# Requesting the out-projection's attention-half weights before the retention's first keys and values

## The chip, the cores and the metric

The kernel runs on one core of a Trainium2 chip. A core has five engines with instruction queues of their own: PE (TensorE, matrix products; PEld in the profile is its loading of weights), DVE (VectorE), ACT (ScalarE), POOL (GpSimd) and SP (SyncE, which here only requests transfers). Sixteen DMA engines move data between the main memory (HBM) and the core's memory (SBUF); transfers are requested by SP and ACT. The metric is the device time of one execution in microseconds (us), lower is better.

## The reference

The program is one layer of a diffusion backbone over 2048 latent tokens (a grid of 32 rows and 64 columns) of width 1024, with 256 context tokens in front. Cut to its core:

```python
h = rmsnorm(x) * (1 + scale) + shift            # scale, shift, gate from SiLU(c) @ w_ada
na_q, na_k, na_v, na_g, r_q, r_k, r_v, r_g = split(h @ w_in)      # latent and context tokens
y_na  = neighbourhood_attention(na_q, na_k, na_v, context, bias) * silu(na_g)   # 8 heads of 64
y_ret = head_rmsnorm(o_forward + o_backward) * silu(r_g)          # 4 heads of 128, chunks of 128
out   = rmsnorm(x + gate * (concat(y_na, y_ret) @ w_out))
```

The retention is computed in chunks: each chunk of 128 tokens gives a state k^T (w v), 128 by 128, where w are decay weights; states are chained forward for one direction and backward for the other. All products of large size are made from numbers split in a high and a low part (three products in place of one), to keep the precision of float32 at a higher rate.

## The kernel before

The kernel runs in stages that overlap on PE: the adaLN vectors and the in-projection; the neighbourhood attention in 128 tiles (8 heads of 16 tiles), between whose products PE does the remaining in-projection steps; then the backward states of the retention (`back_stream`); then the retention's outputs together with the out-projection. What a stage produces goes to HBM (stores, requested by ACT in this part) and is read back by a later one (requests of SP).

Each engine runs its instructions in the order in which the code is written; no scheduler reorders them. The code around the change is written in this order. After the last attention tile, `flush()` issues the stores that are still deferred, among them the last head's y (yS<-y, line 151, on ACT). The attention's memory is given back (`atx.close()`), and `tail_open` (called right then) lays the new pools over it: `wn` first, with two tiles `won0` and `won1` of 16 KB in each of the 128 partitions, then `rp` with the states, then `tb` with three buffers each of keys k4, values v4 and weighed values vw. `won0` lies where the attention's keys were; `won1` lies over the last keys' second half, the context values, the queries and the values. A new tile waits for the last reader or writer of what lay there.

`won0` and `won1` hold the high and low parts of the half of the gated out-projection weights that the attention's y is multiplied with (1024 columns, 512 rows, as four blocks of 128 rows). They are computed earlier and lie in HBM as `woS`. `load_wo(key, k)` requests block k of both: two transfers of 128 by 1024 numbers, 512 KB each. PE reads them first at the beginning of the out-projection (line 1463).

`back_stream` goes through 24 steps: for each of the 4 heads twice the context's two chunks (forward and backward; both share one load), then 16 steps of four chunks. In a step, `ahead(n)` requests the keys and values of step n + 2 (line 1175) and weighs those of step n + 1 on ACT (line 1181); `states` makes one product of 128 by 128 per chunk on PE (line 1187; a float32 product is two instructions on PE); DVE adds it into the chain of states (lines 1217 to 1224). Keys, values and weighed values have three buffers each, so the keys of step n + 3 are requested when the products of step n have read theirs (in the eight context steps, where two steps share a load, correspondingly less often). Between the steps PE makes `fill(8)`, then `fill(3)` or, from the eleventh step on, `fill(2)` steps of the in-projection that were held back: three matmuls for a k-slice, lines 374 and 363. Their outputs are rotated on DVE (lines 402 to 404, 438, 439) with tables (rot) that SP loads too, or copied by ACT (line 449), and stored by ACT (line 151). Before this change, blocks 0 to 3 of the weights are requested at the steps 2, 5, 8 and 11.

A transfer signals its landing on one of eight counters (DMAHW0 to DMAHW7), given out by the program in turn over the requests of SP and ACT. Before an engine requests a transfer on a counter, it waits until the previous transfer on it has landed. So a request can wait for an old transfer that has nothing to do with its data, and all later requests of that engine wait with it.

Of the kernel before, what the change touches and what calls it, by code (L numbers as in the profile page):

```python
# [82 lines left out]
def hybrid_kernel(ctx: ExitStack, tc: tile.TileContext, a: dict, out: bass.AP):  # L83
# [1065 lines left out]
            H["sb"] = rp.tile([P, NCH, P], F32, name=f"sb{H['r']}")  # L1149
        rt["won"] = [wn.tile([P, 4, D], F32R, name=f"won{hl}") for hl in range(2)]  # L1150

    def load_wo(key, k):
        for hl in range(2):
            nc.sync.dma_start(f(rt[key][hl])[:, k % 4, :], woS[hl][k])

    def ret_tables(H):
# [13 lines left out]
    def load_kv(p, H, n0, nn):  # L1170
        r = H["r"]
        res = []
        for src, nm in ((rkS, "k4"), (rvS, "v4")):
            t = p.tile([P, 4, P], F32, name=nm, bufs=4 if nm == "v4" and p is not rt["tb"] else 3)
            nc.sync.dma_start(t[:, :nn, :], src[r // 2][:, r % 2, n0:n0 + nn, :])
            res.append(t)
        return res

    def weigh(p, H, v4, nn, d):
        vw = p.tile([P, 4, P], F32, name="vw")  # L1180
        nc.scalar.activation(vw[:, :nn, :], v4[:, :nn, :], AF.Copy, scale=H["w"][:, d:d + 1])
        return vw

    def states(k4, vw, nn):
        t = ptile(rt["pq"]).rearrange("p (n d) -> p n d", n=4)
        for e in range(nn):
            nc.tensor.matmul(t[:, e, :], k4[:, e, :], vw[:, e, :], start=True, stop=True)  # L1187
        return t

    def back_stream():  # L1190
        rp = rt["rp"]
        back = [(H, NCH, 2, d) for H in HS for d in range(2)]
        back += [(H, 4 * n4, 4, 1) for hp in (HS[2:], HS[:2]) for n4 in range(3, -1, -1) for H in hp]
        kv, vw = {}, {}

        def ahead(n):
            if n + 2 < len(back):
                H, n0, nn, d = back[n + 2]
                kv[n + 2] = kv[n + 1] if n0 == NCH and d == 1 else load_kv(rt["tb"], H, n0, nn)
            if 0 <= n + 1 < len(back):  # L1200
                H, n0, nn, d = back[n + 1]
                vw[n + 1] = weigh(rt["tb"], H, kv[n + 1][1], nn, d)

        ahead(-2)
        ahead(-1)
        yield 1
        for n, (H, n0, nn, d) in enumerate(back):
            ahead(n)
            if n in (2, 5, 8, 11):
                load_wo("won", n // 3)  # L1210
            w, sb = H["w"], H["sb"]
            t = states(kv.pop(n)[0], vw.pop(n), nn)
            if n0 < NCH:
                for e in range(3, -1, -1):
                    m_ = n0 + e
                    if m_ > 0:
                        nc.vector.scalar_tensor_tensor(sb[:, m_ - 1, :], sb[:, m_, :], w[:, 3:4], t[:, e, :], ALU.mult, ALU.add)
            elif d == 0:
                H["sf"] = rp.tile([P, P], F32, name=f"sf{H['r']}", bufs=2)
                nc.vector.tensor_copy(H["sf"], t[:, 0, :])  # L1220
                nc.vector.scalar_tensor_tensor(H["sf"], H["sf"], w[:, 2:3], t[:, 1, :], ALU.mult, ALU.add)
            else:
                nc.vector.tensor_copy(sb[:, NCH - 1, :], t[:, 1, :])
                nc.vector.scalar_tensor_tensor(sb[:, NCH - 1, :], sb[:, NCH - 1, :], w[:, 3:4], t[:, 0, :], ALU.mult, ALU.add)
            yield 1
# [71 lines left out]
    pax.close()  # L1297
    tail_open()
    back = back_stream()
    next(back)  # L1300
    fill(8)
# [194 lines left out]
    for s in range(NJ + 3):  # L1496
        q = plan[s]
        part = [q // 4 + (q % 4 > n) for n in range(4)]
        tick()
        if s >= 4 and s % 4 == 3:  # L1500
            ready.append(s)
        if s + 1 < NJ:
            r_load(J[s + 1])
        if s in (1, 3, 5, 6):
            load_wo("wor", 4 + s // 2)
        if s == 4:
            nc.sync.dma_start(fg, a["final_g_rep"])
        if s == 6:
            nc.gpsimd.tensor_scalar(fg, fg, float(D) ** 0.5, 0.0, ALU.mult, ALU.add)
        if 0 <= s - 3 < NJ:  # L1510
            r_d(J[s - 3])
        if s < NJ:
            r_a(J[s])
        fill(part[0])
        if 0 <= s - 1 < NJ:
            r_b(J[s - 1])
        fill(part[1])
        if 0 <= s - 3 < NJ:
            r_e(J[s - 3])
        fill(part[2])  # L1520
        if 0 <= s - 2 < NJ:
            r_c(J[s - 2])
        fill(part[3])
# [98 lines left out]
```

## Time and profile before

| | before |
|---|---|
| time, median of 3 runs | 1360.26 us (1356.26 to 1361.77) |
| the profiled execution | 1357.68 us, span of its instructions 1355.7 us |
| PE busy | 1310.1 us, 97% |
| PE weight loads | 1146.9 us, 85% |
| DVE, ACT, POOL busy | 61%, 45%, 43% |
| DMA | 287.25 MB, mean 212 GB/s |

The profile is of one execution. Busy time is the time in which an engine had an instruction in work; matmuls are pipelined and their ends are modelled, so a busy PE can still be slowed. The chain of waits follows the work that ended last backwards, at each step to what released it. An SP row (SPq) is a request: its length is the time to issue it, not the transfer. "Idle before" in square brackets is the time for which the engine stood still before an instruction, with what ended it.

### The profile page before, as it was taken

The page shows a single profiled execution, that of the slowest core. Times are in us where ns is not written, and L with a number is a line of the kernel's source. Part 1 is how long each engine was busy: PE and PEld are TensorE (multiplying, and loading weights), DVE is VectorE, ACT ScalarE, POOL GpSimd, SP SyncE. Part 2 cuts the span into 40 slices and gives each one's busy share as a digit, 9 for nine tenths or more (in the row PEclk, how much of TensorE's full clock was granted, in tenths as well). Part 3 has the DMA queues.
Part 4 walks back from the last instruction along what each step waited for, and adds up shares of the span by engine and source line. Part 5 has one row for each costly group of instructions (what it writes and reads, how often), then busy time and mean ns, then how long its engine had stood idle before and what let it go on. Part 6 is the DMA issues. An engine that isn't in the chain of part 4 may idle for free.

```text
span 1355.7 us, 23094 instructions
## 1 busy us (share of the span) xinstructions
PE 1310.1 (97%) x8236; PEld 1146.9 (85%) x8236; DVE 828.3 (61%) x1444; ACT 606.5 (45%) x1259; POOL 579.9 (43%) x569
## 2 busy tenths in 40 slices
PE   6999999999999999999999999999999899999997
PEld 2477899887897788998999889889999789888886
DVE  5687366676766755377767777776654633445345
ACT  4454343343533344455555465556643244333432
POOL 4443101554034664445535474655523154544442
PEclk9999999999999999999999999999999999999999
DMA  9386788464867656978587886666528888555433
GB/s 363 135 279 231 259 313 215 164 210 147 326 182 230 216 203 213 265 210 211 148 225 207 226 224 206 195 181 193 163 90 291 278 290 279 159 163 171 163 121 129
DMA packets 172085, 287.25 MB, mean 212 GB/s; under 512 B 17345, under 2 KB 92225, under 8 KB 170690
## 3 DMA queue, kind: packets, MB, share of 16 engines
q1 hardware_dynamic: 139554, 228.35, 55.8%
q10 hardware_dynamic: 32416, 57.42, 11.8%
q8 instruction: 66, 1.08, 0.3%
q14 instruction: 49, 0.40, 0.1%
HBM read 194.48 MB, written 91.23 MB: 211 GB/s over the span
## 4 chain that ended last, share of the span: by engine, by line
PE 70%; DVE 9%; DMA 8%; POOL 4%; issue 4%; ACT 3%; SPq 1%; ACTq 0%; DVEq 0%; POOLq 0%
PE mm L374 17%; PE mm L671 12%; PE mm L1463 11%; PE mm L363 7%; PE sS L1025 4%; PE tr L1052 3%; PE po L1073 3%; PE mm L1187 2%; PE mm L311 2%; PE tr L1054 2%; PE po L1075 2%; DMA v<-rvS 1%; PE mm L1375 1%; POOL hlo L531 1%; PE mm L1374 1%
## 5 line engine op out<-in xcount | busy, mean ns | idle before, releaser
L374 PE MATMUL mm<-whi,hlo 128*128 128x256 f32 x832 | 228.6, 282 | 1.0 <-DMA hlo<-cS 1.0
L374 PE MATMUL mm<-whi,hhi 128*128 128x256 f32 x768 | 224.3, 292 | 0.0
L374 PE MATMUL mm<-wlo,hhi 128*128 128x256 f32 x768 | 216.8, 282 | 0.0
L1056 ACT CAST pt<-tr 128x640 fp32r<-128x640 f32 (+1 forms) x128 | 95.6, 747 | 160.4 <-PE tr L1054 157.8
L1062 DVE TENSOR_TENSOR pt<-tr,pt 128x640 fp32r<-128x640 f32 (+1 forms) x128 | 114.0, 890 | 78.4 <-ACT pt L1056 77.2
L374 PEld LDWEIGHTS mm<-whi,hlo 128*128 128x128 f32 x832 | 156.6, 191 | 1.4 <-DMA hlo<-cS 1.3
L1045 POOL TENSOR_SCALAR sp<-sp,stt 128x640 f32<-128x640 f32 (+2 forms) x128 | 103.1, 808 | 106.3 <-DVE stt L1044 75.7
L374 PEld LDWEIGHTS mm<-whi,hhi 128*128 128x128 f32 x768 | 146.3, 191 | 0.0
L374 PEld LDWEIGHTS mm<-wlo,hhi 128*128 128x128 f32 x768 | 146.1, 190 | 0.0
L1034 DVE CUSTOM_DVE_ANT_0 sp<-sS,nb 128x640 f32<-128x640 f32 (+2 forms) x128 | 105.6, 825 | 33.4 <-DMA nb<-in_rpb_t_dram 20.7
L1039 ACT ACTIVATE sp<-sp,stt 128x640 f32<-128x640 f32 (+2 forms) x128 | 107.4, 839 | 20.3 <-DVE stt L1034 19.1
L625 POOL TENSOR_TENSOR whi<-st,whi 128x512 fp32r<-128x512 f32 x48 | 62.8, 1330 | 107.7 <-ACT whi L624 107.7
L363 PE MATMUL mm<-hhi,whi 128*128 128x512 f32 x256 | 108.2, 423 | 0.0
L363 PE MATMUL mm<-hlo,whi 128*128 128x512 f32 x256 | 102.0, 399 | 6.0 <-DVE hlo L265 2.1
L1025 PE MATMUL sS<-k,q 128*128 128x256 f32 (+3 forms) x512 | 99.1, 315 | 5.1 <-DVE stt L1034 4.7
L363 PE MATMUL mm<-hhi,wlo 128*128 128x512 f32 x256 | 102.0, 398 | 0.3 <-DVE wlo L347 0.3
L671 PE MATMUL mm<-hhi,whi 128*128 128x512 f32 x336 | 98.1, 395 | 1.6 <-POOL whi L625 1.6
L1463 PE MATMUL mm<-wor,y 128*128 128x512 f32 x384 | 95.7, 398 | 1.1 <-DVE xt L1472 1.1
L1472 DVE TENSOR_TENSOR xt<-mm,xt 128x512 f32<-128x512 f32 x64 | 43.9, 687 | 82.6 <-PE mm L1463 82.5
L1025 PEld LDWEIGHTS sS<-k,q 128*128 128x128 f32 x512 | 82.8, 188 | 12.0 <-DVE stt L1034 8.2
L1463 PE MATMUL mm<-won,y 128*128 128x512 f32 x336 | 89.9, 406 | 0.0
L625 POOL TENSOR_TENSOR wlo<-st,wlo 128x512 fp32r<-128x512 f32 x36 | 53.1, 1476 | 75.8 <-ACT wlo L624 73.7
(258 smaller groups left out, 3051.5 us busy)
## 6 DMA issues: line engine op xcount, KB each, us to landing
st<-in_w_in_dram SPq DMA_DIRECT2D x64, 512.0 KB
q<-qS SPq DMA_DIRECT2D x64, 256.0 KB
hlo<-hS SPq DMA_DIRECT2D x20, 512.0 KB
k<-kS SPq DMA_DIRECT2D x16, 576.0 KB
kS<-o SPq DMA_DIRECT2D x16, 512.0 KB
vB<-o SPq DMA_DIRECT2D x64, 128.0 KB
qS<-o ACTq DMA_DIRECT2D x16, 512.0 KB
woS<-g ACTq DMA_DIRECT2D x32, 256.0 KB
```

Of the source, the lines that this page charges most:

```text
L363: nc.tensor.matmul(pm[:, :n], ww[:, k, cs], h[:, k, :], start=(k == 0 and i == 0), stop=(k == KC - 1 and i == 2))
L374: nc.tensor.matmul(pm[:, t * WG:(t + 1) * WG], h[:, k, o:o + P], ww[:, k, :], start=(k == 0 and i == 0), stop=(k == KC - 1 and i == 2))
L625: nc.gpsimd.tensor_tensor(t[:, 1], r, f(t)[:, 0], ALU.subtract)
L671: nc.tensor.matmul(pm, ww[:, k, :], hh[:, k, :], start=(k == 0 and i == 0), stop=(k == KH - 1 and i == 2))
L1025: nc.tensor.matmul(o, hd["q"][i][:, hl, j * P:(j + 1) * P], k, start=(hl == 0), stop=(hl == 1))
L1034: nc.vector.tensor_tensor_reduce(T["sp"][:, :n], T["s"], nbz[big][:, o:o + n], -1.0, 3e38, ALU.add, ALU.min, T["st"][:, 0:1])
L1039: nc.scalar.activation(sp[:, :n], sp[:, :n], AF.Exp, bias=st[:, 0:1], scale=-1.0, accum_out=st[:, 1:2])
L1045: nc.gpsimd.tensor_scalar(sp[:, :n], sp[:, :n], st[:, 2:3], 0.0, ALU.mult, ALU.add)
L1056: nc.scalar.copy(pt[:, :ng_ + 2, 0, :], tr[:, :ng_ + 2, :])
L1062: nc.vector.tensor_tensor(pt[:, :n, 1, :], tr[:, :n, :], f(pt)[:, :n, 0, :], ALU.subtract)
L1463: nc.tensor.matmul(pm, yy[:, k, :], ww[:, k, sl], start=(k == 0 and i == 0), stop=(k == 3 and i == 2))
L1472: nc.vector.tensor_tensor(xts[t][:, sl], pm, xts[t][:, sl], ALU.add)
```

## The change

All eight requests are taken out of the steps 2, 5, 8 and 11 and placed before the first `ahead`: the four blocks of the high parts first, then the four of the low parts.

```diff
-    def load_wo(key, k):
-        for hl in range(2):
+    def load_wo(key, k, hls=(0, 1)):
+        for hl in hls:
             nc.sync.dma_start(f(rt[key][hl])[:, k % 4, :], woS[hl][k])
...
+        for hl in range(2):
+            for k in range(4):
+                load_wo("won", k, (hl,))
         ahead(-2)
         ahead(-1)
         yield 1
         for n, (H, n0, nn, d) in enumerate(back):
             ahead(n)
-            if n in (2, 5, 8, 11):
-                load_wo("won", n // 3)
```

Only SP's list differs. Before, on SP at the end of attention (k, v: keys and values; rot: rotary tables; the names in brackets are what the request waits for: a counter, or a count of an engine's instructions):

```order
L392 DMA rot<-in_rot_k_dram 128x512 [waits DMAHW4_49]
L1175 DMA k_10725<-rkS_77 128x256 [waits DMAHW1_49,DVE_49,PE_49]
L1175 DMA v_10727<-rvS_79 128x256 [waits DMAHW3_49,DMAHW2_49,Pool_49]
L392 DMA rot<-in_rot_k_dram 128x512
L1175 DMA k_10798<-rkS_77 128x256 [waits DMAHW4_49]
L1175 DMA v_10800<-rvS_79 128x256 [waits DMAHW5_49,DMAHW6_49,DMAHW0_49,DVE_49]
L392 DMA rot<-in_rot_k_dram 128x512
L1175 DMA k_10867<-rkS_78 128x256 [waits DMAHW7_49]
L1175 DMA v_10869<-rvS_80 128x256
L1154 DMA won_10723<-woS_91 128x1024 [waits DMAHW1_49]
L1154 DMA won_10724<-woS_92 128x1024 [waits DMAHW3_49]
```

In this list the second values (v_10800) wait for counter 0, whose last holder is ACT's store of the last y. After the change, at the same place on SP:

```order
L392 DMA rot<-in_rot_k_dram 128x512 [waits DMAHW4_49]
L1154 DMA won_10723<-woS_91 128x1024 [waits DMAHW0_49,PE_49]
L1154 DMA won_10723<-woS_91 128x1024 [waits DMAHW1_49]
L1154 DMA won_10723<-woS_91 128x1024 [waits DMAHW3_49]
L1154 DMA won_10723<-woS_91 128x1024 [waits DMAHW4_49]
L1154 DMA won_10724<-woS_92 128x1024 [waits DMAHW5_49,PE_49]
L1154 DMA won_10724<-woS_92 128x1024 [waits DMAHW6_49]
L1154 DMA won_10724<-woS_92 128x1024 [waits DMAHW7_49]
L1154 DMA won_10724<-woS_92 128x1024 [waits DMAHW0_49]
L1175 DMA k_10733<-rkS_77 128x256 [waits DMAHW1_49,DVE_49]
L1175 DMA v_10735<-rvS_79 128x256 [waits DMAHW2_49,Pool_49]
L392 DMA rot<-in_rot_k_dram 128x512 [waits DMAHW3_49]
```

The eight weight requests (won_10723 high, won_10724 low) now stand ahead of the first keys and values. The count of PE that the first of them waits for is that of the last score product (line 1025); that of the fifth is the last value product (line 1075). The counters have shifted by eight places: counter 2, which the first values (v_10735) take, was held before by ACT's store of the last y.

## Rows read from the trace of the kernel before

**Rows 1.** The page: the chain that ended last, by engine

```profile
PE 70%; DVE 9%; DMA 8%; POOL 4%; issue 4%; ACT 3%; SPq 1%; ACTq 0%; DVEq 0%; POOLq 0%
```

**Rows 2.** The chain in order of time, 1040 to 1097: start, length, what

```profile
1040.89 6.21 DMA v<-rvS
...
1049.59 7.29 DMA v<-rvS
...
1069.04 5.37 DMA v<-rvS
...
1082.84 14.00 PE mm L1463 x59
```

**Rows 3.** Timeline of PE, state products (L1187): start, length, then the idle time

```profile
1039.39 1.05 PE L1187 MATMUL mm<-vw,k 128*128 128x128 f32 x8
...
1045.39 1.05 PE L1187 MATMUL mm<-vw,k 128*128 128x128 f32 x8
...
1050.37 1.05 PE L1187 MATMUL mm<-vw,k 128*128 128x128 f32 x8
1052.65 1.05 PE L1187 MATMUL mm<-vw,k 128*128 128x128 f32 x8
1057.76 1.16 PE L1187 MATMUL mm<-vw,k 128*128 128x128 f32 x8 [2.67 <-ACT vw L1181]
...
1072.11 1.05 PE L1187 MATMUL mm<-vw,k 128*128 128x128 f32 x8
1075.30 1.16 PE L1187 MATMUL mm<-vw,k 128*128 128x128 f32 x8 [0.74 <-ACT vw L1181]
...
1079.98 1.05 PE L1187 MATMUL mm<-vw,k 128*128 128x128 f32 x8
```

**Rows 4.** Timeline of SP: requests from 1012 to 1056

```profile
1012.31 0.33 SPq L1175 DMA_DIRECT2D k<-rkS  x1
...
1017.65 0.32 SPq L1175 DMA_DIRECT2D v<-rvS  x1
...
1038.27 1.91 SPq L1154 DMA_DIRECT2D won<-woS x2
...
1046.89 0.38 SPq L1175 DMA_DIRECT2D v<-rvS  x1
1047.32 0.90 SPq L1154 DMA_DIRECT2D won<-woS x2
...
1055.62 0.32 SPq L1175 DMA_DIRECT2D v<-rvS  x1
```

**Rows 5.** Windows: last columns are granted clock, DMA share and GB/s

```profile
1002.00:1012.00 10.00, 9.96 (x86) 9.75 (x85) 5.20 (x11) 4.00 (x8) 2.79 (x3) 1.00 0.14 42
...
1020.00:1032.00 12.00, 12.00 (x105) 12.00 (x103) 5.31 (x16) 3.68 (x10) 7.17 (x9) 1.00 1.00 355
```

**Rows 6.** Timeline of PE: last scores, last values product, first state product

```profile
1001.62 0.66 PE L1025 MATMUL sS<-k,q 128*128 128x288 f32 x4
...
1011.87 0.40 PE L1075 MATMUL po<-pt,vc 128*128 128x256 f32 x2
...
1018.59 0.61 PE L1187 MATMUL mm<-vw,k 128*128 128x128 f32 x4
```

**Rows 7.** Timeline of ACT: stores requested (ACTq), weighing, copy

```profile
1015.06 0.47 ACTq L151 DMA_DIRECT2D yS<-y  x1
1017.61 0.51 ACT L1181 ACTIVATE vw<-v,w 128x256 f32<-128x256 f32 x1 [4.93 <-DMA yS<-y]
1018.03 0.57 ACT L449 COPY o<-mm 128x512 f32<-128x512 f32 x1
...
1047.28 0.52 ACTq L151 DMA_DIRECT2D rkS<-o  x1
...
1050.23 0.72 ACT L1181 ACTIVATE vw<-v,w 128x512 f32<-128x512 f32 x1 [1.04 <-DMA v<-rvS]
```

**Rows 8.** What SP waited for, 1050 to 1057: in total, times, longest

```profile
SPq L1175 <- DMA rkS<-o: 3.8, 1, 3.8
```

## The prediction

> **What bounds the kernel now.** I read the chain of waits first, then the starts of the products on PE in the stretch that the change touches, then the requests of SP and the DMA load there.
>
> PE sets the end: its instructions make up 70% of the chain of waits, DMA 8% [rows 1]. Around the change PE ends attention, makes eight steps of the in-projection and then the 24 steps of state products (two instructions to a product, four products to a full step) with projection steps between them; there the chain passes three times through a transfer of values, v<-rvS: 6.21, 7.29 and 5.37 us [rows 2]. These lengths are not losses: PE has other steps meanwhile. What is lost shows in the starts of the state products. I number the steps 0 to 23; step 8, the first with four products, starts at 1039.39, step 10 at 1045.39 and step 23 at 1079.98 [rows 3]. From step 10 on a step with nothing to wait for takes 2.28 us (1050.37 to 1052.65), so 13 steps want 29.64 us and took 34.59: **4.95 us are lost**. Steps 10 to 14 (1045.39 to 1057.76) took 12.37 for 9.12, so 3.25 of it lie there, where a pair of weight transfers was requested at 1038.27 and another at 1047.32 [rows 4]. Steps 14 to 23 took 22.22 for 20.52: 1.70 are lost with no weights on the way, 0.91 of it at step 21 (3.19 for 2.28, from 1072.11 to 1075.30). PE's granted clock is 1.00, the upper of its two levels (2.4 GHz), in each window read here, so a wait costs its own length alone [rows 5].
>
> **The change part by part.** It moves eight requests of SP and nothing else. No instruction on PE, ACT, DVE or POOL is added or moved, and the bytes are the same: eight times 512 KB, 4.2 MB.
>
> *The four high parts.* In the change's list the first waits only for PE: the room is that of the last keys, whose last reader is the score product that starts at 1001.62 and takes 0.66 [rows 6]. So they go out from 1002.3. SP's next request in the list before waited until 1012.31 [rows 4], so nothing on SP is queued behind them in that time. The DMA engines are free: share 0.14 from 1002 to 1012 [rows 5]. Where they are full they move 355 GB/s (1020 to 1032) [rows 5], so 2.1 MB take 5.9 us; with about 2.2 us from request to first landing they are in by 1010.4. The 2.2 is worked out: the 128 KB store that ACT requests at 1015.06 releases ACT at 1017.61, which is 2.55 less 0.37 for its bytes [rows 7]. Cost: nothing; idle DMA engines hide them. Without that cover they would cost what the next part costs.
>
> *The four low parts.* The first waits for the last value product, which starts at 1011.87 and takes 0.40 [rows 6]: from 1012.3, the moment at which the list before requests the first keys [rows 4]. Another 2.1 MB. These requests are for weights in rows of 4 KB, so I take 380 GB/s, a little over the 355 of a mixed stretch, and 5.5 us: landed by 1012.3 + 2.2 + 5.5 = 1020.0. Behind them on SP stand all keys, values and rotary tables of the state steps. Before, this traffic was spread over 1019 to 1056, where DMA had to carry it too; now it stands in front of step 0.
>
> *The wait that is added.* The first values take counter 2 in the change's list, and its last holder is ACT's store of attention's last y, requested at 1015.06 [rows 7]. In the list before it was the second values that waited for this store, and the trace shows it: SP requests v at 1017.65, just when that store's landing releases ACT too, 1017.61 [rows 4, 7]. Now the first values cannot be requested before the store has landed, and the store has 2 MB of weights ahead of it. That such a store is slow beside weights the trace shows: the values requested at 1055.62 had waited 3.8 us for a store rkS<-o [rows 4, 8] which ACT had requested at 1047.28 [rows 7], 8.3 us before, beside a weight pair. Taking transfers of both queues in the order of their requests: weights in at 1020.0, keys (128 KB, 0.35) and store (0.35) by 1020.7; values requested, 2.5 us as above, at 1023.2; the weighing on ACT 0.1 + 0.51 [rows 7], PE 0.05 later: step 0 starts at 1023.85 instead of 1018.59 [rows 6]. **The head loses 5.2 us**, all of it PE idle, since PE's list is fixed and stands at step 0. Bounds: below, the values lie behind the weights in SP's own queue whatever the store does, 1020.0 + three times 0.35 for keys, store and values + 0.66 = 1021.7, that is 3.1; above, the store takes 8.3 us as at 1047.28, landing at 1023.4, and the loss is 7.9. I take 5.2, in between, because the weights ahead (about 2 MB) are all that is in flight, and SP adds nothing behind them while it waits.
>
> *What waits behind it.* ACT stands at the first weighing, so the copy of a finished projection tile, which began at 1018.03 and took 0.57, moves with it [rows 7]. It will end some 0.5 us after step 0 has begun, where before it ended with it (1018.60 and 1018.59 [rows 6]). PE needs that buffer for its next tile, and the products of step 0 alone take 0.61 [rows 6], so I count nothing. Rotary tables and the second to fourth values are requested right after the first, into an empty queue: nothing. Steps 0 to 9 lose nothing more; they lost nothing with the weights in their traffic.
>
> *What goes.* Steps 11 and 14 had values behind a weight pair: the transfer of 7.29 us [rows 2] was requested at 1049.59 behind the pair of 1047.32 [rows 4]. Without a pair ahead, values requested at 1046.89 were weighed from 1050.23, 3.3 us later [rows 4, 7]. A buffer comes round every three steps: 6.84 less the 1.05 of the product gives 5.8 us for two requests (0.4), transfer (3.3 to 4.6) and weighing (0.8), 4.5 to 5.8. So steps 11 to 14 fit, and I take their 3.25 us as gained. What is late next is the same loop with the stores and rotary tables of the last steps, 1.70, which I leave. Bounds: 0, if the loop loses as much without weights; 4.95, if all of it goes.
>
> *Sum.* +5.2 − 3.25 = +1.95 us. From 1082.84 the chain is PE's out-projection [rows 2], so what remains moves the end one for one. The profiled execution took 1357.68 us (span 1355.7 and 2.0 around it); the sum makes it 1359.6. The median of the runs is 1360.26, 2.6 above it; on that scale **1362.2 us**.
>
> **A rule of the Trainium skill.** The trace has a store landing 8.3 us after its request beside weights [rows 7, 8]. The Trainium skill, DMA: Bandwidth & Descriptors, section "Queues, rings and completion order", says that each DMA engine takes turns between the queues of SP and ACT, one packet from each; the same section says that a completion count lands only after all earlier writes of that engine, over its queues. By the first half the store would not wait for the weights, and the sum would be the second case below; by the second half it would come in about the order that I took. The 8.3 us speak for the second.
>
> **The rivals.**
> - *The two queues take turns.* The store lands at about 1015.06 + 2.2 + 0.75 = 1018.0, the values go into SP's queue behind the remaining weights, and the head loses the lower bound, 3.1. With 3.25 gained: 1360.1; with all 4.95 gone: 1358.4. For it: the light store took 2.55 us [rows 7]. Against it: the wait of 3.8 [rows 8].
> - *Slower: the loop of three buffers is the limit, not the weights.* If the keys and values of a step alone fill the loop, steps 11 to 23 lose 4.95 as before, the head is paid in full, and the time is 1365.5. For it: 1.70 are lost over nine steps without weights. Against it: 3.25 over four steps beside them. It decides once the gain falls under 5.2; with the head at its upper bound too, it is 1368.2.
> - *The early requests are not early.* If the high parts too went out only at 1012.3, step 0 would stand behind 4.2 MB: head 5.2 + 5.5 = 10.7, time 1367.7. Against it: the last reader of the keys at 1001.62 and SP idle until 1012.31 [rows 4, 6].
>
> **How the numbers follow.** Forecast 57%, turns 25%, the loop 12%, not early 3%, anything else 3%. A measurement of this kernel tells about 0.5% from no change, 1353.5 to 1367.1. The forecast, the turns and the loop at its middle lie inside; outside above are the loop with the upper head, a late start, and scatter (9%); outside below only scatter, since 4.95 us is all there is to gain and the head costs at least 3.1 (4%). The range takes the turns with everything gone below (1358.4, less 2 for the scatter of medians: the three runs span 1356.26 to 1361.77) and the loop above (1365.5, plus 1): 1356.5 to 1366.5.
>
> **What would show it.** In the trace after: DMA share of about 0.7 from 1002 to 1012; SP's first keys at about 1014 and first values only at 1018 to 1023, waiting for yS<-y; before step 0 a PE idle time of 3 to 8 us ended by the weighing on ACT; DMA almost idle at about 1022; steps 10 to 14 at 2.3 us each. Wrong is the head if step 0 starts before 1021; wrong is the gain if from step 10 to step 23 more than 32.5 us pass; wrong is the whole if the time leaves 1353.5 to 1367.1.

## The result and the profile after

The changed kernel takes 1362.23 us in the median of 20 runs (1359.81 to 1364.79); the kernel before, run beside it, took 1359.58 (20 runs, 1355.16 to 1362.97). The ratio is 1.0023 with a 95% interval of 1.0013 to 1.0033: 3.1 us slower (the two medians lie 2.65 apart), inside the 0.5% that the prediction calls no change, and larger than the 1.95 us that it worked out. That the 1362.2 predicted and the 1362.23 measured agree to the digit is chance: the kernel before was 0.7 us faster beside the change than in the runs shown earlier. Two repetitions gave 1.0026 and 1.0027, so by these ratios the change costs 3.1 to 3.7 us.

The profiled execution took 1364.52 us with a span of 1362.5. Not all of the 6.8 us more belongs to the change: the last score product, behind which the first weights are requested, and attention's last values product, which in the trace of before start at 1001.62 and 1011.87 [rows 6], both start later here:

```profile
1003.57 0.66 PE L1025 MATMUL sS<-k,q 128*128 128x288 f32 x4
...
1013.83 0.40 PE L1075 MATMUL po<-pt,vc 128*128 128x256 f32 x2
```

The later start lies ahead of the first moved request; between the two rows pass 10.26 us, for 10.25 before. Over the traces of this study the last values product's second instruction lies between 1011.9 and 1016.1, at 1016.04 and at 1011.94 in two kernels that are alike up to there; it is scatter of the stages ahead. So I compare traces from this instruction on (1012.00 before, 1013.95 after), and times by their ratios. Of the 6.8 us, 1.95 lie ahead of it, 4.5 in the stretch that follows and 0.3 behind that.

The page's chain by engine, for [rows 1], has DMA at 10% for 8%, of which the head below is 8.45 us or 0.6%; it also takes another way through the stages ahead of the change:

```profile
PE 62%; DMA 10%; DVE 10%; POOL 6%; issue 6%; ACT 4%; SPq 1%; ACTq 1%; POOLq 0%; DVEq 0%
```

**The head.** SP's list after, with the requests of the weights, the first keys and the first values, answers to [rows 4]:

```profile
1004.26 11.74 SPq L1154 DMA_DIRECT2D won<-woS  x8
1016.10 0.68 SPq L1175 DMA_DIRECT2D k<-rkS  x1
1023.55 0.32 SPq L1175 DMA_DIRECT2D v<-rvS  x1
```

What SP waited for between 1000 and 1100 (line, releaser: total, times, longest) names both waits within the weights and the one of the values:

```profile
SPq L1154 <- PE sS L1025: 9.2, 1, 9.2
SPq L1154 <- PE po L1075: 8.2, 1, 8.2
SPq L1175 <- DMA yS<-y: 6.7, 1, 6.7
```

So four requests go out when the last scores are done, four more 8.2 us later when the last values product is done, and then the values wait 6.7 us for the store of attention's last y, as their counter says. The chain of waits runs through exactly these:

```profile
1017.01 6.47 DMA yS<-y
...
1023.55 1.98 DMA v<-rvS
...
1025.55 0.52 ACT vw L1181
...
1026.11 1.22 PE mm L1187 x4
1027.34 3.31 PE mm L374 x18
...
1031.09 2.15 PE mm L374 x18
```

The store, 128 KB, lands 6.47 us after its request, where it took 2.55 in the trace before [rows 7]. The packets of the two queues (number, MB, share of the 16 engines) say why. From 1017.0 to 1020.5, right behind its request, only SP's queue, q1, has any; ACT's, q10, has its first from 1020.5 to 1021.5:

```profile
q1 hardware_dynamic: 361, 1.31, 100.7%
...
q10 hardware_dynamic: 27, 0.05, 13.7%
```

Before, all 80 packets of the store start from 1016.5 to 1017.5 (the row below), the first 1.5 us after the request; here the first comes 3.85 us after it:

```profile
q10 hardware_dynamic: 80, 0.13, 34.7%
```

So the data of the store is late, and not only the report of its landing. ACT's rows (its idle time in brackets) and PE's state products show what stands behind it:

```profile
1025.55 0.51 ACT L1181 ACTIVATE vw<-v,w 128x256 f32<-128x256 f32 x1 [10.92 <-DMA v<-rvS]
1025.96 0.57 ACT L449 COPY o<-mm 128x512 f32<-128x512 f32 x1
```

```profile
1026.11 1.22 PE L1187 MATMUL mm<-vw,k 128*128 128x128 f32 x4 [5.41 <-ACT vw L1181]
1030.48 0.61 PE L1187 MATMUL mm<-vw,k 128*128 128x128 f32 x4
1033.09 0.60 PE L1187 MATMUL mm<-vw,k 128*128 128x128 f32 x4
...
1054.69 1.05 PE L1187 MATMUL mm<-vw,k 128*128 128x128 f32 x8
...
1063.81 1.05 PE L1187 MATMUL mm<-vw,k 128*128 128x128 f32 x8
...
1071.65 1.16 PE L1187 MATMUL mm<-vw,k 128*128 128x128 f32 x8 [0.83 <-ACT vw L1181]
...
1081.78 1.16 PE L1187 MATMUL mm<-vw,k 128*128 128x128 f32 x8 [0.74 <-ACT vw L1181]
...
1086.45 1.05 PE L1187 MATMUL mm<-vw,k 128*128 128x128 f32 x8
```

The shown steps are 0, 1, 2, 10, 14, 17, 21 and 23. PE stands for 5.41 us before step 0, which comes 12.16 us after the last values product (1026.11 less 1013.95) where before it came after 6.59 (1018.59 [rows 6] less 1012.00): **the head lost 5.57 us**. Then comes a loss that the prediction does not have. Step 0 to step 1 takes 4.37 us where a context step takes 2.60 (1030.48 to 1033.09): the two products of step 0 last 1.22 for 0.61, and 18 in-projection matmuls 3.31 for 2.15 in the chain. The windows show why (columns as in the first line; the granted clock stands before the DMA share):

```profile
core 0: us, PE busy (x) PEld busy (x) DVE busy (x) ACT busy (x) POOL busy (x), PEclk, DMA share, GB/s
1002.00:1012.00 10.00, 9.96 (x85) 9.75 (x84) 5.56 (x14) 5.59 (x11) 2.79 (x3) 1.00 0.68 243
...
1016.00:1020.00 4.00, 4.00 (x36) 4.00 (x35) 0.00 (x0) 0.00 (x0) 0.98 (x1) 1.00 1.00 374
1021.00:1023.00 2.00, 0.00 (x0) 0.00 (x0) 0.00 (x0) 0.00 (x0) 0.00 (x0) 1.00 0.48 179
1023.00:1025.00 2.00, 0.00 (x0) 0.00 (x0) 0.00 (x0) 0.00 (x0) 0.00 (x0) 0.51 0.14 47
1025.00:1027.00 2.00, 0.89 (x5) 0.89 (x5) 0.00 (x0) 1.45 (x4) 0.04 (x1) 0.50 0.88 268
1027.00:1029.00 2.00, 2.00 (x11) 2.00 (x11) 0.64 (x2) 2.00 (x8) 2.00 (x3) 0.50 0.93 188
1029.00:1031.00 2.00, 2.00 (x16) 2.00 (x15) 1.07 (x4) 1.19 (x4) 2.00 (x4) 0.79 0.63 223
1031.00:1033.00 2.00, 2.00 (x19) 2.00 (x19) 0.89 (x4) 0.00 (x0) 2.00 (x4) 1.00 0.41 112
```

From about 1023 PE's granted clock is 0.50, the lower of its two levels (1.2 GHz), and PE, once it has work again, works at it until about 1030: 11 matmuls in the 2 us from 1027 for 19 in those from 1031. From step 0 to step 10 pass 28.58 us for 26.80 before (1045.39 less 1018.59 [rows 3, 6]): **1.78 us lost to the clock**, all of it before step 1.

**The gain.** Steps 10 to 14 take 9.12 us (1054.69 to 1063.81), 2.28 each: nothing is lost there any more. Steps 14 to 23 take 22.64 for 22.22. Together 31.76 for 34.59 [rows 3]: **2.83 us gained**. In the sum of this trace, 5.57 + 1.78 − 2.83 = +4.52.

### The profile page after: what moved, and what is told of

The parts are those of the page before. It is cut to its first block, busy times and chain, and to the rows that moved or that the text cites. A ratio compares the mean times of both kernels' runs of the same rounds, so it can differ in the third digit from the quotient of the medians.

```text
span 1362.5 us, 23092 instructions
## 1 busy us (share of the span) xinstructions
PE 1310.3 (96%) x8236; PEld 1148.8 (84%) x8236; DVE 830.7 (61%) x1444; ACT 606.2 (44%) x1259; POOL 580.7 (43%) x569
## 4 chain that ended last, share of the span: by engine, by line
PE 62%; DMA 10%; DVE 10%; POOL 6%; issue 6%; ACT 4%; SPq 1%; ACTq 1%; POOLq 0%; DVEq 0%
PE mm L374 13%; PE mm L1464 11%; PE mm L671 8%; PE mm L363 7%; PE sS L1025 4%; PE tr L1052 3%; PE po L1073 3%; PE mm L1187 2%; PE tr L1054 2%; PE mm L311 2%; PE po L1075 2%; DMA ggS<-o 1%; POOL g L759 1%; POOL hlo L531 1%; DMA woS<-g 1%
## 5 line engine op out<-in xcount | busy, mean ns | idle before, releaser
L1034 DVE CUSTOM_DVE_ANT_0 sp<-sS,nb 128x640 f32<-128x640 f32 (+2 forms) x128 | 105.5, 824 | 33.8 <-DMA nb<-in_rpb_t_dram 21.1
```

What stands on the lines that cost most here:

```text
L1034: nc.vector.tensor_tensor_reduce(T["sp"][:, :n], T["s"], nbz[big][:, o:o + n], -1.0, 3e38, ALU.add, ALU.min, T["st"][:, 0:1])
```

## The experiments

Each short diff is against the changed kernel. The columns of the table: start of step 0 after the second instruction of the last values product, with PE's idle time in it; steps 0 to 10; steps 10 to 23; from that values product to the first out-projection product (line 1464 after), the sum that the change moves; all in us, from one trace each. Then the ratio of times to the kernel before, run beside it, with its interval.

| run | to step 0 (idle) | 0 to 10 | 10 to 23 | whole stretch | ratio of times |
|---|---|---|---|---|---|
| before | 6.59 (0) | 26.80 | 34.59 | 70.27 | 1 |
| the change | 12.16 (5.41) | 28.58 | 31.76 | 74.78 | 1.0023 (1.0013 to 1.0033) |
| the change, again | 11.94 (5.19) | 28.87 | 31.28 | 74.37 | 1.0026 (1.0010 to 1.0042) |
| the change, a third time | 11.09 (4.34) | 29.60 | 31.28 | 74.25 | 1.0027 (1.0015 to 1.0038) |
| high early, low in the steps | 6.59 (0) | 26.80 | 31.00 | 66.68 | 0.9985 (0.9975 to 0.9995) |
| low early, high in the steps | 9.52 (2.77) | 28.26 | 30.75 | 70.82 | 1.0016 (1.0005 to 1.0027) |
| low as two transfers | 9.63 (2.88) | 28.38 | 30.29 | 70.59 | 1.0020 (1.0010 to 1.0030) |
| low as two transfers, again | 9.75 (3.00) | 28.39 | 31.17 | 71.60 | 1.0008 (0.9996 to 1.0019) |
| high early, low at odd steps | 6.59 (0) | 26.80 | 30.54 | 66.22 | 0.9982 (0.9969 to 0.9995) |
| more work before step 0 | 13.79 (0) | 19.60 | 30.62 | 66.29 | 0.9974 (0.9961 to 0.9986) |
| low behind the first values | 6.59 (0) | 33.24 | 31.17 | 73.28 | 1.0002 (0.9989 to 1.0014) |
| products in the wait | 11.33 (0.78) | 27.02 | 30.76 | 71.46 | 1.0019 (1.0009 to 1.0029) |

Traces and times agree only roughly. Against before, the stretch differs by −3.59 us with the high parts alone early, +0.55 with the low parts alone, +0.32 in the first trace with two transfers and +3.01 with the low parts behind the values, while the times differ by −2.0, +2.2, +2.7 and +0.3; each of these four traces lies outside the interval of its times. One trace is one execution: the same kernel's stretch differed by 1.0 us between two traces (two transfers), and of the kernel before there is one trace alone.

### One half of the change at a time

```diff
-        for hl in range(2):
-            for k in range(4):
-                load_wo("won", k, (hl,))
+        for k in range(4):
+            load_wo("won", k, (0,))
...
+            if n in (2, 5, 8, 11):
+                load_wo("won", n // 3, (1,))
```

> Only the four high parts are requested early; the low parts go out one each at steps 2, 5, 8 and 11, as in the kernel before. My theory (the head is paid for the low parts in front of the first values and for the store's counter; the gain comes from weights taken out of the traffic of steps 10 to 23): PE waits under 0.5 us before step 0, its clock stays at 1.00, steps 10 to 23 take about 33 us, between 34.6 (before) and 31.8 (the change), and the time is 0.9990 of before (0.9980 to 1.0000). Rival (any weights requested before the first keys and values delay them): an idle PE of 2 us or more before step 0 and a time of 1.001 or more.

Measured: step 0 after 6.59 us with no idle time, exactly as before; steps 10 to 23 in 31.00, less than expected; the time 0.9985, 2.0 us faster. SP waited 1.3 us for the store at the second values, as in the order before:

```profile
SPq L1175 <- DMA yS<-y: 1.3, 1, 1.3
```

So the high parts by themselves cost nothing and bring the gain, 3.59 us in the trace; the head is paid for the low parts alone. The gain needs only one of each pair to go: with 0.5 MB in the steps in place of 1 MB, steps 10 to 14 took 9.24 us.

The other half swaps the numbers, `(1,)` early and `(0,)` in the steps.

> The mirror image: the four low parts early, the high parts one each at steps 2, 5, 8 and 11. Here the first values take a counter that is free, so they are requested at about 1015 us, but they stand behind 2.1 MB in SP's queue. My theory (the queue makes most of the head, the counter the rest): PE waits 3 to 4.5 us before step 0, less than the 5.4 of the change; steps 10 to 23 take about 33 us; time 1.001 of before (0.9998 to 1.0025). Rival (the counter alone makes the head): PE waits under 1 us and the time is 0.999 or below.

Measured: step 0 after 9.52 us with 2.77 of idle time, a little under the 3 expected, and steps 10 to 23 in 30.75 for about 33 expected. The first values are requested at 1016.19, without a wait for the store; the second values wait for the store (SP's wait, then step 0 on PE with its idle time):

```profile
SPq L1175 <- DMA yS<-y: 4.2, 1, 4.2
```

```profile
1022.65 1.22 PE L1187 MATMUL mm<-vw,k 128*128 128x128 f32 x4 [2.77 <-ACT vw L1181]
```

2.93 us of head are the price of 2 MB in front of the first keys and values when the first values have not to wait for the store. This is the prediction's lower bound, 3.1.

### The low parts with two counters fewer

```diff
-                load_wo("won", k, (hl,))
+        for k in (0, 2):
+            nc.sync.dma_start(f(rt["won"][1])[:, k:k + 2, :], woS[1][k:k + 2].rearrange("k p d -> p k d"))
```

Two requests of 1 MB for four of 512 KB (the high parts as in the change): the same bytes at the same place, but six requests in place of eight take counters in turn ahead of the first values, which no longer get the one that the store holds.

> The change with one thing altered: the low parts are requested as two transfers of 1 MB instead of four of 512 KB. The same bytes stand in front of the first values, but the counters shift by two places and the first values no longer take the counter of the last y's store (the second keys do). My theory: the first values are requested before 1018 us (1023.5 in the change) and land with the end of the weights, PE waits about 4 us instead of 5.4, and if its clock holds the 1.7 us after it go too; steps 10 to 23 as in the change, 31.8; time 1.0005 of before (0.9993 to 1.0018). Rival (the counter costs nothing, the weights in the queue are all): PE waits 5 us or more and the time is 1.0023, that of the change.

> The version with two low transfers of 1 MB once more, beside the change. My theory: 9.4 to 9.9 us again from the last values product to step 0, and a time 1 to 3 us under the change in this call. Rival (the counter is nothing): 11.5 us or more to step 0 in this execution; or the same 9.6 us and a time like the change's, in which case the time is lost elsewhere, by the clock or ahead of the stage, and the trace has to say where.

Measured: step 0 after 9.63 and 9.75 us, heads of 3.04 and 3.16 in place of 5.57, 5.35 and 4.50 in the three traces of the change; now the second keys have the counter and wait for it in the values' place (4.7 us in the first trace, 4.8 in the second):

```profile
SPq L1175 <- DMA yS<-y: 4.7, 1, 4.7
```

That the transfers are larger here is not the reason: the low parts alone, in four requests of 512 KB and without that wait, lost 2.93. Of the head, then, about 3 us are the weights ahead, and the other 1.3 to 2.5 the wait of the first values for the store. The times do not tell the two kernels apart: 1.0020, above the range that was expected, then 1.0008, against 1.0023 to 1.0027, with intervals that overlap. The wait is shown by the traces alone.

> The change itself once more, beside the next kernel on one chip, since the first pair disagreed: in the traces the version with two low transfers waits 2.5 us less before step 0, in the timed runs the two medians are alike. My theory (the head is fixed by the store's counter): 12.0 to 12.4 us again from the last values product to step 0, SP waiting 6 to 7 us for the y store; how much the lower clock adds after it differs from run to run (0 to 2 us). Time 1.0015 to 1.0035 of before. Rival (the first trace was an odd one): under 11 us to step 0.

> The change once more, beside the run with products in the wait, to compare the two on one chip: idle of 5.2 to 5.4 us before step 0, steps 0 to 10 in 28.6 to 28.9, ratio to before 1.0025 if it is as it was (1.0023 and 1.0026).

Measured: heads of 5.35 and 4.50 us, 31.28 from step 10 to 23 in both, and 2.07 and 2.80 lost between steps 0 and 10; the idle time of the third trace, 4.34, is under the 5.2 that was expected. The three traces of the change sum to +4.5, +4.1 and +4.0 us.

### What hides the head, and what the clock costs

```diff
         ahead(-2)
+        yield 1
         ahead(-1)
-        yield 1
...
-    fill(8)
+    fill(18)
...
-        fill(3 if n < 10 else 2)
+        fill(2)
```

Ten of the in-projection steps held back stand before step 0 now, in place of one behind each of the first ten; the first weighing moves behind them in the lists; all eight requests are where the change has them.

> The change, with ten more held-back projection steps in front of step 0 (18 in place of 8, and two in place of three behind each of the first ten steps, so the total is the same), and the first weighing moved behind them on ACT. My theory (the head is PE standing at step 0 of a fixed list, with nothing else wrong): the wait before step 0 falls under 1 us, the clock stays at 1.00, steps 10 to 23 take 30 to 32 us, time 0.998 of before (0.9968 to 0.9992). Rival (the head moves: with less projection between the first steps, their keys and values come late instead): steps 0 to 10 lose 2 us or more and the time is 1.000 or above.

Measured: the first values wait for the store as in the change, 6.0 us:

```profile
SPq L1175 <- DMA yS<-y: 6.0, 1, 6.0
```

But PE has work of its own until step 0, reaches it after 13.79 us and finds the weighed values there; no idle time, clock 1.00. The stretch takes 66.29 us, 3.98 less than before, and the time is 0.9974 (0.9961 to 0.9986), 3.5 us faster than before. In this kernel the late values cost nothing, since PE had work for as long as they took.

Here the wait is kept and the idle time filled with work that does nothing:

```diff
-    def states(k4, vw, nn):
+    def states(k4, vw, nn, dummy=0):
...
+        for e in range(dummy):
+            nc.tensor.matmul(t[:, 2 + e % 2, :], ident, ident, start=True, stop=True)
...
-            t = states(kv.pop(n)[0], vw.pop(n), nn)
+            t = states(kv.pop(n)[0], vw.pop(n), nn, 17 if n == 0 else 0)
```

> The changed kernel with 17 products of the identity with itself (34 PE instructions, about 0.13 us each by the trace, 4.6 us in all) ahead of step 0's own; their results go to a part of the buffer that nobody reads. Nothing else differs, so the first values come as late as in the change and step 0 starts at the same distance from the last values product (12.0 us, give or take 0.3). If the low granted clock after the idle time is what makes steps 0 to 10 longer, PE no longer stands idle for long, the clock stays at 1.00, and steps 0 to 10 take 26.8 us again in place of 28.6 to 28.9; the time falls by 1.8 us against the change, ratio to before about 1.001. Rival, the steps are longer because keys, values and rotary tables come late behind the store and the weights: steps 0 to 10 take 28.6 as in the change, and the time is the change's, 1.0025.

Measured (here the products of states are on line 1189, the idle ones on 1187):

```profile
1021.85 3.96 PE L1187 MATMUL mm<-ident 128*128 128x128 f32 x34
1026.59 0.71 PE L1189 MATMUL mm<-vw,k 128*128 128x128 f32 x4 [0.78 <-ACT vw L1181]
1029.31 0.71 PE L1189 MATMUL mm<-vw,k 128*128 128x128 f32 x4
```

Windows of this kernel, and of the change in the run beside it:

```profile
1024.00:1026.00 2.00, 1.81 (x17) 1.62 (x15) 0.00 (x0) 0.00 (x0) 0.00 (x0) 1.00 0.50 95
1026.00:1028.00 2.00, 1.41 (x12) 1.41 (x13) 0.62 (x2) 1.97 (x6) 0.56 (x1) 1.00 0.76 257
```

```profile
1022.00:1024.00 2.00, 0.49 (x2) 0.49 (x3) 0.00 (x0) 1.05 (x3) 0.00 (x0) 0.68 0.94 261
1024.00:1026.00 2.00, 2.00 (x11) 2.00 (x11) 0.64 (x2) 2.00 (x7) 1.63 (x3) 0.50 0.86 245
```

Step 0 comes as late as in that run of the change (11.33 and 11.09 us), but the clock stays at 1.00, and steps 0 to 10 take 27.02 us for 29.60. The rival, late keys and tables, has no room left in 0.2 us. In that stretch the clock is shown as the cause, and its price is 1.8 to 2.8 us over the three traces of the change. It follows how long PE worked at the lower level, from step 0 to the clock's return in the windows: about 3.7, 4.4 and 6.0 us, of which 1.78, 2.07 and 2.80 were lost, nearly half each time. So the trace with the shortest head lost most behind it, and head and clock together came to 7.35, 7.42 and 7.30 us. The whole time fell by less than the 1.8 us expected, from 1362.76 to 1362.1, with intervals that overlap; after the stretch this one trace is 1 us and more longer than all others (275.5 us from the first out-projection product to the end, the others 273.4 to 274.5), which I can't explain. The other executions point the same way: their mean granted clocks average 0.9946, 0.9945 and 0.9951 over the runs of the change, 0.9962 with the products in the wait and 0.9957 to 0.9965 for the kernel before. How many microseconds it takes from the median stays open.

### Other places for the low parts

```diff
-        for hl in range(2):
-            for k in range(4):
-                load_wo("won", k, (hl,))
+        for k in range(4):
+            load_wo("won", k, (0,))
...
+            if n in (1, 3, 5, 7):
+                load_wo("won", n // 2, (1,))
```

> High parts early, low parts one each at steps 1, 3, 5 and 7, before the steps with four products begin. My theory: no head, and the whole gain of the change, since no weights are left in the traffic of steps 10 to 23: PE idle under 0.5 us before step 0, steps 10 to 23 in 31.5 to 32.3 us, time 0.9979 of before (0.9970 to 0.9990). Rival (the gain in steps 10 to 23 came from the loads having a lead over PE after the head, not from the missing weights): steps 10 to 23 take 33.5 us or more and the time is that of before.

Measured: nothing lost up to step 10, steps 10 to 14 in 9.12, steps 10 to 23 in 30.54 and so less than expected, the stretch 66.22 us, the time 0.9982 (0.9969 to 0.9995). Here step 0 is not late, so the gain in steps 10 to 23 does not come from a lead that the loads get by the head: that rival fell.

```diff
+        for k in range(4):
+            load_wo("won", k, (0,))
         ahead(-2)
         ahead(-1)
+        for k in range(4):
+            load_wo("won", k, (1,))
```

> The smallest mend: high parts early as in the change, the four low parts right behind the first keys and values instead of in front of them. My theory (only what stands in front of the first values is paid): PE idle under 0.5 us before step 0; the second values now stand behind 2 MB, but are wanted 5.2 us later, so at most 1 us is lost at step 2; steps 10 to 23 in 30 to 32 us; time 0.9982 of before (0.9970 to 0.9995). Rival (any 2 MB in this place is paid, by whichever values come next): 2 us or more lost at step 2 or 4, and a time of 1.000 or above.

Measured: the theory fell, and what its rival forecast came. The first values are in time and step 0 does not wait, but the second values, requested at 1021.00, take 7.86 us behind the low parts, and step 2 stands:

```profile
1021.00 7.86 DMA v<-rvS
...
1028.88 0.52 ACT vw L1181
...
1029.44 1.22 PE mm L1187 x4
1030.66 3.76 PE mm L374 x18
```

```profile
1026.00:1028.00 2.00, 0.00 (x0) 0.00 (x0) 0.00 (x0) 0.00 (x0) 1.33 (x2) 0.84 1.07 387
1028.00:1030.00 2.00, 0.56 (x2) 0.56 (x3) 0.00 (x0) 0.91 (x2) 0.00 (x0) 0.50 0.73 217
```

The four low requests hold counters too: SP's requests of keys and values waited 4.2 us in all, three times, for landings of weights. Steps 1 to 3 lose 6.44 us (33.24 less 26.80): 4.22 before step 2, the rest at the low clock behind it (step 2 to 3 takes 4.82 for 2.60). In one piece the low parts cost something before the values, and in this trace behind the first of them too. By the trace the stretch is 3.0 us longer than before, by the times the kernel is level (1.0002). The traced execution, 1363.22 us, was the slowest of the twelve, whose median is 1359.56, and the mean clocks of the twelve go from 0.993 to 0.998; so the usual execution may lose less than this one. That is not shown.

## Why the prediction was right, and where it was not

**Which case it was.** The forecast: slower by little, within 0.5%, with a head lost and the four steps beside the weights gained.

**High parts free: right.** DMA share 0.68 from 1002 to 1012 (0.7 expected), no idle time on PE, and attention's end no longer for it: from the last score product to the last values product 10.26 us for 10.25. With the high parts alone early the head is that of before, 6.59 us.

**The head, 5.2 us: right, and by the steps it named.** Measured 5.57, 5.35 and 4.50. The first values waited for the store, the store came behind the weights (6.47 us for 128 KB), PE stood until the weighing. That the size fits so well is in part luck: in the first trace the values were requested about 0.9 us later than the 1020.7 worked out (1021.6 on the scale of before), and then took 1.98 us for 2.5. The lower bound, 3.1, is what the two kernels without that wait of the first values lost (2.93; 3.04 and 3.16). Taken from the last values product, SP's first keys came at 1014.15 and its values at 1021.6 on the scale of the trace before (1.95 us off each), inside the forecast's 1014 and 1018 to 1023.

**The gain, 3.25 us: right.** Steps 10 to 14 take 9.12 us in the three traces of the change, 3.25 less than 12.37, as worked out. Steps 14 to 23, left at 22.22, took 22.64, 22.16 and 22.16: that loss was the loop's own, and without weights it stays in the change. In the other kernels these steps took 21.1 to 22.1 us, so it is not fixed. One half of the weights away is enough for most of it (9.24 and 9.68).

**The step that failed: "a wait costs its own length alone".** It was read off windows in which PE was busy, and so was "Steps 0 to 9 lose nothing more". They lost 1.78, 2.07 and 2.80 us, because PE's clock fell to the lower level in the new idle time and came back only 3.7 to 6.0 us after step 0 had begun. With 1.8 for it, the prediction's sum would have been +5.2 + 1.8 − 3.25 = +3.75; the traces give +4.0 to +4.5, the times +3.1 to +3.7. That it was missing did not change the case, but it is about as large as the whole sum that was forecast.

**The rivals.** *The two queues take turns*: fell; the store did not land near 1018.0 but 6.47 us after its request, and for the 3.5 us shown above SP's queue moved 361 packets and ACT's none. The same holds in all eight traces with the low parts ahead of the store: its first packet comes 3.8 to 4.0 us after the request, and 1.4 to 1.5 us after it in the four others. The rule of the Trainium skill (DMA: Bandwidth & Descriptors, "Queues, rings and completion order") that a completion count lands only after earlier writes of that engine over its queues, by which the prediction explained the order, does not explain it: the store's packets themselves start late, so these traces do not test that rule, and why the packets start late no run here tells. *The loop of three buffers is the limit*: fell; steps 10 to 14 lose nothing. *Early not early*: fell; the high parts went out 8.2 us ahead of the low ones.

## What to carry to other kernels

When room comes free early, ask how many bytes the idle transfer engines can take in before the next urgent load: here the high half of the weights was free and by itself brought the whole gain, the low half stood in front of the first keys and values and cost more than it brought. Where requests share completion counters, count which old transfer the first urgent request now falls behind; here a store of 128 KB behind a burst of weights took 5.3 to 6.5 us for 2.55. And an idle time of PE is to be priced with what the clock may cost behind it. Held-back work placed into it removed both here; that version has the lowest ratio, 0.9974, though its interval overlaps those of the two kernels at 0.9982 and 0.9985.

## What had not been expected of the hardware

That the granted clock falls in an idle time, or right behind one, is plain in these traces; when it does is not. In the trace of before PE stands 2.67 us ahead of step 14 [rows 3], and the clock stays at its upper level in that time and behind it:

```profile
1055.00:1057.00 2.00, 0.09 (x1) 0.00 (x0) 1.38 (x5) 0.02 (x1) 1.26 (x1) 1.00 0.47 138
1057.00:1059.00 2.00, 1.25 (x10) 1.20 (x11) 0.05 (x1) 1.27 (x2) 0.00 (x0) 1.00 0.86 310
```

With the low parts early alone, 2.77 us of idle time before step 0 were followed by the lower level:

```profile
1022.50:1025.00 2.50, 2.35 (x11) 2.35 (x12) 0.64 (x2) 2.50 (x9) 1.49 (x3) 0.50 0.82 229
```

So were 2.88 and 3.00 us with the low parts as two transfers (the second time the clock fell only when PE had been at work again for 0.7 us), 4.06 in the kernel with the low parts behind the values, and 4.34 to 5.41 in the change; the idle time of 0.78 us with products in the wait was not. What sets 2.67 us apart from 2.77, the kind of work before, the moment or the length, no run here tells.
